# Where the operand tiles begin in SBUF: 32 bytes more among the constants, and the tiny tiles in a pool of their own at the end

## The chip, the cores and the metric

The kernel runs on one core of a Trainium2 chip. The metric is the device time of one launch, in microseconds. TensorE (PE) multiplies, its weight loads (PEld) run beside it, VectorE (DVE), ScalarE (ACT) and GpSimd (POOL) work on tiles in SBUF and PSUM, and SyncE (SP) issues nearly all DMAs. SBUF has 128 partitions; a tile takes the same stretch of bytes in each of them, and "begins at" below always means the byte within a partition.

## The reference, cut to what matters

Two blocks of two layers each run one after the other on one sequence of 256 tokens with 1024 features, all in float32.

```python
def first_block(x, ...):                     # layer 0: differential attention, layer 1: neighbourhood attention
    h = x
    for i in range(2):
        h = h + mixer_i(rmsnorm(h, norm_mix[i]))
        h = h + swiglu(rmsnorm(h, norm_ffn[i]), w_gate[i], w_up[i], w_down[i])        # hidden width 2816
        gate = sigmoid(rmsnorm(h, norm_ple[i]) @ ple_w_gate[i])
        h = h + gate * (p[i] @ ple_w_proj[i])
    return rmsnorm(h, norm_final)

def second_block(x, ...):                    # layer 0: convolution and pooling, layer 1: forgetting and block attention
    h = x
    for l in range(2):
        h = h + mixer_l(rmsnorm_2(h, mix_norm_g[l]))
        h = h + conv_ffn(rmsnorm_2(h, ffn_norm_g[l]), ...)                            # hidden width 2816
    return rmsnorm_2(h, final_norm_g)

reference = second_block(first_block(x, ...), ...)
```

The sequence is so short that the weights rule everything: some 220 MB of them are read once, and each is multiplied with 256 tokens.

## The kernel before

**Products.** Activations lie feature-major: a tile `u_both` of 128 partitions holds eight feature tiles, each with a high and a low half of 256 tokens. A float32 product is made of three matmuls on the type float32r: high by high, high by low, low by high (`mm3`). A line of the program that issues a matmul is always L195, in the helper `mm`; groups are told apart by the tile they write. The second operand named there is held in the array (stationary), the third streams through it (moving).

- `out_tile` and `pair` write `ps_g`: weights stationary, `u_both` moving, eight feature tiles of three matmuls with 256 columns.
- `wide_tile`, used by both feed-forward kinds, writes `ps_w`: for each feature tile one matmul of 512 columns (weights' high half by both halves of `u_both`) and one of 256 (weights' low half by the high half of `u_both`). The pair covers the 768 columns of an `mm3`.
- `Acc.step` writes `acc`: weights stationary, moving either `u_both` (after attention and in the mixer of the second block) or `m`, the middle of a feed-forward.
- `ps_v` has `u_both` stationary and the weights moving.
- Attention has small products (`ps_S`, `ps_V`) and transposes (`ps_t`, `ps_r`, `ps_V<-ident`), in which the tile `ident` is moving.

**Weights.** `Weights.load` sends a 512 KB piece by DMA into one of five `stage` tiles; `Weights.split` makes its high half on ACT (L88) and its low half on DVE (L89) into one of eight `w_both` tiles; `take` hands over the next one.

**Order.** Loops in Python write the program in its final order. Attention steps that would make PE wait are put off by a counter (`at`, `tick`), so that other matmuls stand between. Each engine runs its own queue in that order and waits for semaphores.

**Layout.** Pools lie one after the other in SBUF in the order in which they are opened: `const`, `stage`, `split` (the `w_both` tiles), `acts` (`u_both`) and `work`. Inside a pool tiles follow each other in the order of their first use, each size rounded up to 32 bytes. No tile is placed by hand. What this gives, worked out from the sizes in the program (the remainder on division by 512 bytes, and by 64):

| tiles | begin at, mod 512 | mod 64 |
|---|---|---|
| `h`, `ct`, `off` (in `const`) | 128, 128, 384 | 0 |
| `ident`, `tri` (in `const`) | 256 | 0 |
| `ug0`, `ug1`, `ug2` (in `const`) | 384, 416, 448 | 0, 32, 0 |
| `stage`, `w_both`, `u_both`, and of `work`: `sc`, `t2`, `bias`, `ssq`, `q`, `k`, `v`, `on` | 480 | 32 |
| `m`, `q_both`, `k_both`, `pool_m`, `R` (in `work`, behind the 32-byte tile `rstd`) | 32 | 32 |
| `a`, `sums`, `z`, `at` (in `work`, behind the 32-byte tiles `st`) | 160 | 32 |

All slices that a matmul of the large products reads begin a multiple of 512 bytes behind its tile's start, so they have the tile's remainder. One small product is an exception: `pz` has 264 columns, its moving slices of `w_both` lie 1056 bytes apart, and they begin at 480, 0 and 32 mod 512 in turn; its stationary slices of `u_both` begin at 480.

**What the change touches.** The pool list in `network` (L110 to L116), the constants (L177 on), and the places that take a tiny tile: `rstd_a` (`rstd`), `softmax_pair` and `da_steps` (`st`), `qkv_group` (`zf`), `fox_prepare` (`ft`, `lf`, `fc`).

Of the kernel before, what the change touches and what calls it, by code (L numbers as in the profile page):

```python
# [10 lines left out]
F32 = mybir.dt.float32  # L11
# [95 lines left out]
def network(ctx: ExitStack, tc: tile.TileContext, x_t, p_t, cols, b_v, na_bias, t5_bias, w_mats, out):  # L107
    nc = tc.nc

    const = ctx.enter_context(tc.tile_pool(name="const", bufs=1))  # L110
    stage = ctx.enter_context(tc.tile_pool(name="stage", bufs=N_STAGE))
    split = ctx.enter_context(tc.tile_pool(name="split", bufs=N_HI))
    acts = ctx.enter_context(tc.tile_pool(name="acts", bufs=2))
    work = ctx.enter_context(tc.tile_pool(name="work", bufs=2))
    psum = ctx.enter_context(tc.tile_pool(name="psum", bufs=1, space=PSUM))
    pass  # L116


    chunks = []
# [46 lines left out]
    for _ in range(N_STAGE - 1):  # L166
# [6 lines left out]
    dist = work.tile([128, 2, S], F32, tag="sc", bufs=3, name="dist")  # L173
    nc.gpsimd.iota(dist, pattern=[[-128, 2], [1, S]], base=0, channel_multiplier=-1,
                   allow_small_or_imprecise_dtypes=True)
    ones = const.tile([128, 1], F32, name="ones")
    nc.gpsimd.memset(ones, 1.0)  # L177
    mhalf = const.tile([128, 2], F32, name="mhalf")
# [91 lines left out]
    def rstd_a(n, eps=1e-6):  # L270
        ps = psum.tile([128, 4], F32, tag="m", bufs=2, name="ps_ss")
        two = hasattr(n, "ssq2")
        mean_square(ps[:, 0:2], n.ssq, getattr(n, "end", None))
        if two:
            mean_square(ps[:, 2:4], n.ssq2)
        st = work.tile([128, 8], F32, tag="rstd", name="rstd")
        n.rstd = st[:, 0:2]
        nc.vector.tensor_scalar(st[:, 2:4], ps[:, 0:2], 1.0 / D, eps, op0=OP.mult, op1=OP.add)  # L278
        nc.gpsimd.tensor_tensor(n.rstd, st[:, 2:4], mhalf, op=OP.pow)  # L279
        if two:  # L280

            nc.vector.tensor_mul(st[:, 4:6], n.rstd, n.rstd)
            nc.vector.scalar_tensor_tensor(st[:, 4:6], ps[:, 2:4], 1.0 / D, st[:, 4:6], op0=OP.mult, op1=OP.mult)
            nc.vector.tensor_scalar(st[:, 4:6], st[:, 4:6], eps, None, op0=OP.add)
            nc.gpsimd.tensor_tensor(st[:, 6:8], st[:, 4:6], mhalf, op=OP.pow)
            nc.vector.tensor_mul(st[:, 6:8], st[:, 6:8], n.rstd)
            n.both = st[:, 6:8]
        else:
            n.both = n.rstd
# [17 lines left out]
    def bc2(r):  # L307
        return r[:, None, :].to_broadcast([128, 2, S])
# [106 lines left out]

    def softmax_pair(sc, ps, bias, widths):

        st = work.tile([128, 8], F32, tag="st", bufs=4, name="st")
        for i in range(2):
            nc.vector.tensor_tensor_reduce(sc[:, i, :widths[i]], ps[:, i, :widths[i]], bias[i], 1.0, FLOOR,  # L420
                                           OP.add, OP.max, st[:, i:i + 1])
        nc.vector.tensor_scalar(st[:, 2:4], st[:, 0:2], -1.0, None, op0=OP.mult)  # L422
        for i in range(2):
            nc.scalar.activation(sc[:, i, :widths[i]], sc[:, i, :widths[i]], AF.Exp,  # L424
                                 bias=st[:, 2 + i:3 + i], accum_out=st[:, 4 + i:5 + i])
        nc.vector.reciprocal(st[:, 6:8], st[:, 4:6])
        return st

    def qkv_group(n, g, kind, bv, steps):
        q = work.tile([128, 2, S], F32, tag="q", bufs=1, name="q")  # L430
        k = work.tile([128, 2, S], F32, tag="k", bufs=1, name="k")

        def parts(x, tag):
            both = work.tile([128, 2, 2, S], F32R, tag=tag + "2", name=tag + "_both")
            hi = both[:, :, 0, :]
            nc.scalar.activation(hi, x, AF.Copy)
            nc.vector.tensor_sub(both[:, :, 1, :], x, hi.bitcast(F32))
            return x, both

        v = work.tile([128, 2, S], F32, tag="v", name="v")  # L440
        u = n.u
        ps = pair(u)
        if kind == "na":
            t = work.tile([128, 2, S], F32, tag="qb", bufs=1, name="qb")
            nc.vector.tensor_mul(t, ps, bc2(n.R))
            for i in range(2):
                nc.scalar.activation(q[:, i, :], t[:, i, :], AF.Identity, bias=b_q8[:, 2 * g + i:2 * g + i + 1],
                                     scale=0.125)
        else:
            nc.vector.scalar_tensor_tensor(q, ps, 0.125, bc2(n.R), op0=OP.mult, op1=OP.mult)  # L450
        q = parts(q, "q")
        ps = pair(u)
        if kind == "na":
            t = work.tile([128, 2, S], F32, tag="qb", bufs=1, name="kb")
            nc.vector.tensor_mul(t, ps, bc2(n.R))
            for i in range(2):
                nc.scalar.activation(k[:, i, :], t[:, i, :], AF.Identity, bias=col("b_k", 2 * g + i), scale=1.0)
        else:
            nc.vector.tensor_mul(k, ps, bc2(n.R))
        k = parts(k, "k")  # L460
        steps(q, k, v)
        if kind == "od" and g == 0:
            z = work.tile([128, 2, 8], F32, tag="zf", bufs=1, name="zf")
            pz = [psum.tile([128, 264], F32, tag=f"acc{2 + t}", name="pz") for t in range(2)]
            kk = 0
            for n_k in (3, 3, 2):
                w = W.take(n_k * 264)
                for i in range(n_k):
                    for t in range(2):
                        for a, b in ((0, 0), (1, 0), (0, 1)):  # L470
                            mm(pz[t], u[:, kk, a, t * 128:(t + 1) * 128], w[:, b, i * 264:(i + 1) * 264],
                               kk == 0 and (a, b) == (0, 0), kk == 7 and b == 1)
                    kk += 1
                    if kk % 2 == 0:
                        tick()
            for t in range(2):
                nc.scalar.activation(v[:, t, :], pz[t][:, :256], AF.Copy, scale=n.rstd[:, t:t + 1])
                nc.vector.scalar_tensor_tensor(z[:, t, :], pz[t][:, 256:264], n.rstd[:, t:t + 1],
                                               ct[:, COL["b_f"]:COL["b_f"] + 8], op0=OP.mult, op1=OP.add)
            fox_prepare(z, extra)  # L480
            return
        pv = psum.tile([128, 2, S], F32, tag="acc3", name="ps_v")
        for half in range(2):
            w = W.take(1024)
            for i in range(4):
                kk = 4 * half + i
                for t in range(2):
                    mm3(pv[:, t, :], u[:, kk, :, t * 128:(t + 1) * 128], w[:, :, i * 256:(i + 1) * 256],
                        kk == 0 and t == 0, kk == 7)
                if i % 2 == 1:  # L490
                    tick()
        for t in range(2):
            if kind == "na":
                nc.vector.scalar_tensor_tensor(v[:, t, :], pv[:, t, :], n.rstd[:, t:t + 1], bv,
                                               op0=OP.mult, op1=OP.add)
            else:
                nc.scalar.activation(v[:, t, :], pv[:, t, :], AF.Copy, scale=n.rstd[:, t:t + 1])
# [38 lines left out]
    def da_steps(g, q, k, v, bias, o, emitted):  # L536
        for p in range(2):
# [23 lines left out]
            def values(p=p, box=box):  # L561
                po = att_psum("V")
                at = box["at"]
                for qt in range(2):
                    for kk in range(2):
                        mm(po[:, qt * 128:(qt + 1) * 128], at[:, kk * 256 + qt * 128:kk * 256 + (qt + 1) * 128],
                           v[:, kk, p * 128:(p + 1) * 128], kk == 0, kk == 1)
                st = work.tile([128, 8], F32, tag="st", bufs=4, name="st2")
                dump = work.tile([128, 128], F32, tag="dump", bufs=1, name="dump")
                for qt in range(2):  # L570
                    nc.scalar.activation(dump, po[:, qt * 128:(qt + 1) * 128], AF.Square, accum_out=st[:, qt:qt + 1])
# [122 lines left out]
    extra = {}  # L694

    def fox_prepare(z, extra):
        zz = z.rearrange("p a b -> p (a b)")
        t = work.tile([128, 3, 16], F32, tag="ft", bufs=1, name="ft")
        nc.vector.tensor_scalar(t[:, 0, :], zz, -1.0, None, op0=OP.mult)
        nc.vector.tensor_tensor(t[:, 0, :], t[:, 0, :], zz, op=OP.min)  # L700
        nc.scalar.activation(t[:, 1, :], t[:, 0, :], AF.Exp)
        nc.scalar.activation(t[:, 1, :], t[:, 1, :], AF.Ln, bias=1.0)
        nc.vector.tensor_scalar(t[:, 2, :], zz, 0.0, None, op0=OP.min)
        lf = work.tile([128, 2, 8], F32, tag="lf", bufs=1, name="lf")
        nc.vector.tensor_sub(lf.rearrange("p a b -> p (a b)"), t[:, 2, :], t[:, 1, :])

        def cum():
            ps = psum.tile([128, 2, 8], F32, tag="m", bufs=2, name="ps_f")
            mm(ps[:, 0, :], tri, lf[:, 0, :], True, True)
            mm(ps[:, 1, :], ones.to_broadcast([128, 128]), lf[:, 0, :], True, False)  # L710
            mm(ps[:, 1, :], tri, lf[:, 1, :], False, True)
            extra["f"] = work.tile([128, 2, 8], F32, tag="fc", bufs=1, name="fc")
            nc.vector.tensor_copy(extra["f"], ps)

        cum()
# [394 lines left out]
```

## Time and profile before

| | us |
|---|---|
| median of 3 runs | 1292.58 (1291.73 to 1294.84) |
| the profiled execution's own time | 1291.94 |
| its span in the profile | 1290.1 |
| PE busy | 1260.4, 98% |
| DVE busy | 995.7, 77% |
| ACT busy | 755.1, 59% |
| POOL busy | 32.6, 3% |

The span is what the records cover; the rest of the profiled execution's time, 1.84 us, lies around it. PE is busy from start to end, with weight loads hidden beside it, so the pace at which one matmul follows another is the quantity to read. A matmul's recorded duration (280 to 400 ns) is longer than that pace, since matmuls overlap in the pipeline; the pace comes from the chain of work that ended last, which names for each run of matmuls its start, its length up to the next piece, and its count: length by count is the pace. Where a row of the timeline gives a run of n matmuls, its length holds n - 1 paces and one full duration. Columns of float32r at TensorE's full clock of 2.4 GHz take 0.4167 ns each, 256 of them 106.7 ns, 768 of them 320 ns, if one goes in per cycle.

### The profile page before, as it was taken

Reading aid. Unit: us, or ns where it says so; the run is one execution under the profiler, and the core shown is the slowest. Engines: PE = TensorE matmul, PEld = TensorE weight load, DVE = VectorE, ACT = ScalarE, POOL = GpSimd, SP = SyncE. Lnnn points to the kernel's source line nnn. Section 1 sums busy time; section 2 is a strip of 40 time slices with the busy share of each in tenths; the row PEclk is TensorE's granted clock in tenths of the full one; section 3 lists DMA queues with packets and bytes.
Section 4 is the critical chain, followed back from the end, with each engine's and each line's share of the span. In section 5 each row is a group of like instructions: output and inputs, shape, how many; then the busy total and the mean of one; then the engine's idle time right before and its main releaser. Section 6 shows DMA issues by size and latency. Waiting matters only on the chain.

```text
span 1290.1 us, 23187 instructions
## 1 busy us (share of the span) xinstructions
PE 1260.4 (98%) x9040; PEld 1165.1 (90%) x9040; DVE 995.7 (77%) x1884; ACT 755.1 (59%) x1354; POOL 32.6 (3%) x54
## 2 busy tenths in 40 slices
PE   6999999999999999999999999999999999999997
PEld 6999899999989998999999998999999898899997
DVE  7876877777876667777788889888886766888884
ACT  6776655555666565555567456555665565655563
POOL 1000000000010000000000000000000000000000
PEclk9999999999999999999999999999999999999998
DMA  8554666664757436566546475666645343566640
GB/s 281 157 160 147 186 191 193 191 183 147 230 167 189 130 116 213 192 191 187 180 140 204 127 244 168 191 187 191 186 151 192 99 131 131 180 193 185 193 133 34
DMA packets 62926, 222.30 MB, mean 172 GB/s; under 512 B 7264, under 2 KB 7776, under 8 KB 62688
## 3 DMA queue, kind: packets, MB, share of 16 engines
q1 hardware_dynamic: 60768, 214.52, 53.6%
q0 software_dynamic: 1616, 5.77, 1.9%
q8 instruction: 71, 1.16, 0.4%
q10 hardware_dynamic: 432, 0.53, 0.1%
q14 instruction: 39, 0.32, 0.1%
HBM read 219.74 MB, written 1.05 MB: 171 GB/s over the span
## 4 chain that ended last, share of the span: by engine, by line
PE 91%; DVE 4%; issue 1%; POOL 1%; DMA 1%; ACT 1%; SPq 0%; POOLq 0%; DVEq 0%; ACTq 0%
PE ps_w L195 36%; PE acc L195 24%; PE ps_g L195 16%; PE ps_v L195 5%; PE ps_S L195 3%; PE ps_V L195 2%; PE ps_t L394 1%; DVE w_both L89 1%; DVE u_both L256 1%; PE ps_p L195 1%; POOL rstd L279 1%; DVE h L372 1%; DVE ssq L247 1%; DMA stage<-w_da_qkv 1%; ACT w_both L88 1%
## 5 line engine op out<-in xcount | busy, mean ns | idle before, releaser
L89 DVE TENSOR_TENSOR w_both<-stage,w_both 128x1024 fp32r<-128x1024 f32 (+2 forms) x413 | 495.3, 1201 | 123.8 <-ACT w_both L88 122.1
L88 ACT ACTIVATE w_both<-stage 128x1024 fp32r<-128x1024 f32 (+2 forms) x413 | 427.7, 1037 | 174.8 <-issue 55.3
L195 PE MATMUL ps_w<-u_both,w_both 128*128 128x512 f32 (+1 forms) x2816 | 504.4, 339 | 1.0 <-DVE u_both L256 1.0
L195 PEld LDWEIGHTS ps_w<-u_both,w_both 128*128 128x128 f32 x2816 | 431.1, 189 | 63.7 <-DVE u_both L256 2.3
L195 PE MATMUL ps_g<-u_both,w_both 128*128 128x256 f32 x1920 | 254.0, 289 | 8.0 <-ACT w_both L88 7.5
L195 PE MATMUL acc<-m,w_both 128*128 128x256 f32 x2112 | 255.8, 280 | 0.0
L195 PEld LDWEIGHTS acc<-m,w_both 128*128 128x128 f32 x2112 | 251.5, 188 | 1.8
L195 PEld LDWEIGHTS ps_g<-u_both,w_both 128*128 128x128 f32 x1920 | 238.5, 193 | 12.3 <-ACT w_both L88 7.5
L340 ACT ACTIVATE sums<-ps_w 128x256 f32<-128x256 f32 x176 | 67.6, 384 | 197.0 <-PE ps_w L195 197.0
L341 DVE TENSOR_TENSOR sums<-ps_w,sums 128x256 f32<-128x256 f32 x176 | 74.2, 422 | 54.1 <-ACT sums L340 53.7
L195 PE MATMUL acc<-u_both,w_both 128*128 128x256 f32 x768 | 98.2, 286 | 0.4 <-DVE u_both L585 0.4
L195 PEld LDWEIGHTS acc<-u_both,w_both 128*128 128x128 f32 x768 | 93.8, 192 | 2.1 <-DVE u_both L585 0.6
L195 PE MATMUL ps_v<-w_both,u_both 128*128 128x256 f32 x528 | 70.7, 287 | 0.0
L195 PEld LDWEIGHTS ps_v<-w_both,u_both 128*128 128x128 f32 x528 | 65.4, 191 | 3.3 <-issue 1.5
L424 ACT ACTIVATE sc<-sc,st 128x256 f32<-128x256 f32 (+1 forms) x96 | 46.0, 482 | 17.2 <-DVE st L422 17.2
L731 ACT ACTIVATE t<-sums 128x256 f32<-128x256 f32 x88 | 36.6, 416 | 18.4 <-DVE sums L762 15.0
L254 ACT ACTIVATE u_both<-h,ct 128x256 fp32r<-128x256 f32 x72 | 32.3, 497 | 16.7 <-DVE h L372 14.9
L734 DVE SCALAR_TENSOR_TENSOR t<-t,sums 128x256 f32<-128x256 f32 x88 | 37.4, 425 | 2.8
L279 POOL TENSOR_TENSOR rstd<-rstd,mhalf 128x2 f32<-128x2 f32 x11 | 12.2, 1105 | 1079.3 <-DVE rstd L278 1079.3
L735 ACT ACTIVATE m<-t 128x256 fp32r<-128x256 f32 x88 | 35.7, 406 | 3.5 <-DVE t L734 3.4
L256 DVE SCALAR_TENSOR_TENSOR u_both<-h,ct,u_both 128x256 fp32r<-128x256 f32 x72 | 31.6, 480 | 7.9 <-ACT u_both L254 7.9
L736 DVE TENSOR_TENSOR m<-t,m 128x256 fp32r<-128x256 f32 x88 | 36.9, 419 | 1.0 <-ACT m L735 1.0
(164 smaller groups left out, 843.2 us busy)
## 6 DMA issues: line engine op xcount, KB each, us to landing
stage<-w_gu SPq DMA_DIRECT2D x88, 512.0 KB, 3.7
stage<-w_in SPq DMA_DIRECT2D x88, 512.0 KB, 4.0
stage<-w_down SPq DMA_DIRECT2D x44, 512.0 KB, 3.7
stage<-w_out SPq DMA_DIRECT2D x44, 512.0 KB, 4.1
stage<-w_na_qkv SPq DMA_DIRECT2D x24, 512.0 KB, 4.6
stage<-w_da_qkv SPq DMA_DIRECT2D x23, 512.0 KB, 4.9
stage<-w_od_in SPq DMA_DIRECT2D x22, 512.0 KB, 4.2
stage<-w_gate SPq DMA_DIRECT2D x16, 512.0 KB, 3.6
```

The source lines that it names most:

```text
L88: self.nc.scalar.activation(hi[:, s], t[:, s], AF.Copy)
L89: self.nc.vector.tensor_sub(lo[:, s], t[:, s], hi[:, s].bitcast(F32))
L195: nc.tensor.matmul(o, a, b, start=start, stop=stop, **kw)
L254: nc.scalar.activation(n.u[:, 2 * b + i, 0, :], src[:, i, :], AF.Copy, scale=gain(2 * b + i))
L256: nc.vector.scalar_tensor_tensor(n.u[:, 2 * b + i, 1, :], src[:, i, :], gain(2 * b + i), n.u[:, 2 * b + i, 0, :].bitcast(F32), op0=OP.mult ...
L340: nc.scalar.activation(out, ps[:, 1, :], AF.Copy)
L341: nc.vector.tensor_add(out, ps[:, 0, :], out)
L424: nc.scalar.activation(sc[:, i, :widths[i]], sc[:, i, :widths[i]], AF.Exp, bias=st[:, 2 + i:3 + i], accum_out=st[:, 4 + i:5 + i])
L731: nc.scalar.activation(t, g, AF.Tanh, scale=0.5)
L734: nc.vector.scalar_tensor_tensor(mf, a, 0.5, other, op0=OP.mult, op1=OP.mult)
L735: nc.scalar.activation(m[:, 0, :], mf, AF.Copy)
L736: nc.vector.tensor_sub(m[:, 1, :], mf, m[:, 0, :].bitcast(F32))
```

## The change

A 32-byte tile `pad` is added among the constants and filled with zeros, and nothing reads it. With it the constants end 32 bytes later, at a multiple of 512 bytes, and so `stage`, `w_both`, `u_both` and `work` begin there. The tiles of 32 to 192 bytes leave `work` for a new pool `small` behind it, with the same tags and numbers of buffers. All larger tiles of `work` then begin at multiples of 512 bytes. The constants behind `pad` move by 32 bytes: `ident` and `tri` from 256 to 288 mod 512, `ug0`, `ug1`, `ug2` from 384, 416, 448 to 416, 448, 480. `h`, `ct` and `off` stay.

```diff
@@ network
     work = ctx.enter_context(tc.tile_pool(name="work", bufs=2))
+    small = ctx.enter_context(tc.tile_pool(name="small", bufs=2))
     psum = ctx.enter_context(tc.tile_pool(name="psum", bufs=1, space=PSUM))
-    pass
...
+
+    pad = const.tile([128, 8], F32, name="pad")
+    nc.gpsimd.memset(pad, 0.0)
     ones = const.tile([128, 1], F32, name="ones")
     nc.gpsimd.memset(ones, 1.0)
@@ rstd_a
-        st = work.tile([128, 8], F32, tag="rstd", name="rstd")
+        st = small.tile([128, 8], F32, tag="rstd", name="rstd")
@@ softmax_pair
-        st = work.tile([128, 8], F32, tag="st", bufs=4, name="st")
+        st = small.tile([128, 8], F32, tag="st", bufs=4, name="st")
@@ qkv_group
-            z = work.tile([128, 2, 8], F32, tag="zf", bufs=1, name="zf")
+            z = small.tile([128, 2, 8], F32, tag="zf", bufs=1, name="zf")
@@ da_steps
-                st = work.tile([128, 8], F32, tag="st", bufs=4, name="st2")
+                st = small.tile([128, 8], F32, tag="st", bufs=4, name="st2")
@@ fox_prepare
-        t = work.tile([128, 3, 16], F32, tag="ft", bufs=1, name="ft")
+        t = small.tile([128, 3, 16], F32, tag="ft", bufs=1, name="ft")
...
-        lf = work.tile([128, 2, 8], F32, tag="lf", bufs=1, name="lf")
+        lf = small.tile([128, 2, 8], F32, tag="lf", bufs=1, name="lf")
...
-            extra["f"] = work.tile([128, 2, 8], F32, tag="fc", bufs=1, name="fc")
+            extra["f"] = small.tile([128, 2, 8], F32, tag="fc", bufs=1, name="fc")
```

The order of instructions and their waits on PE, DVE, ACT and SP is the same in both programs. Only POOL's queue gets one instruction more, near its start. POOL before, from the second iota to the first DMA:

```order
8 L174 IOTA dist 128x512
9 L177 MEMSET ones 128x1
10 L179 MEMSET mhalf 128x2
11 L181 MEMSET zero_102 128x16
12 L183 IOTA rcnt 128x64
```

POOL after, the same stretch:

```order
8 L174 IOTA dist 128x512
9 L178 MEMSET pad 128x8
10 L180 MEMSET ones 128x1
11 L182 MEMSET mhalf 128x2
12 L184 MEMSET zero_107 128x16
13 L186 IOTA rcnt 128x64
```

The memset of `pad` stands ahead of `ones`; everything behind it on POOL comes one place later and is otherwise unchanged.

## Rows read from the trace of the kernel before

**Rows 1.** The page's part 1: busy time, share of the span, instructions by engine.
```profile
PE 1260.4 (98%) x9040; PEld 1165.1 (90%) x9040; DVE 995.7 (77%) x1884; ACT 755.1 (59%) x1354; POOL 32.6 (3%) x54
```

**Rows 2.** Waits of PE, the longest in total: microseconds, times, longest.
```profile
PE ps_r L295 <- POOL rstd L279: 8.3, 9, 2.5
```

**Rows 3.** Groups of PE's matmuls, shapes apart: count, busy, mean ns, idle before.
```profile
L195 PE MATMUL ps_w<-u_both,w_both 128*128 128x512 f32 x1408 | 497.8, 398 | 1.0 <-DVE u_both L256 1.0
L195 PE MATMUL ps_w<-u_both,w_both 128*128 128x256 f32 x1408 | 392.8, 280 | 0.0
L195 PE MATMUL acc<-m,w_both 128*128 128x256 f32 x2112 | 255.8, 280 | 0.0
L195 PE MATMUL ps_g<-u_both,w_both 128*128 128x256 f32 x1920 | 254.0, 289 | 8.0 <-ACT w_both L88 7.5 <-DVE w_both L89 0.5
L195 PE MATMUL acc<-u_both,w_both 128*128 128x256 f32 x768 | 98.2, 286 | 0.4 <-DVE u_both L585 0.4
L195 PE MATMUL ps_v<-w_both,u_both 128*128 128x256 f32 x528 | 70.7, 287 | 0.0
...
L195 PE MATMUL ps_V<-v,at 128*128 128x128 f32 x64 | 8.6, 278 | 0.0
...
L394 PE MATMUL ps_t<-ident,a 128*128 128x128 f32 x32 | 5.1, 272 | 0.0
```

**Rows 4.** Chain that ended last, pieces in order: start us, length us, what xcount.
```profile
152.07 5.44 PE acc L195 x48
...
202.33 5.66 PE acc L195 x48
207.98 11.11 PE ps_w L195 x64
...
523.46 11.30 PE ps_w L195 x64
...
716.72 15.95 PE ps_g L195 x133
732.67 1.18 PE ps_pool L195 x10
...
753.14 15.86 PE acc L195 x132
```

**Rows 5.** The same chain, asked for 488.6 to 491.3 alone.
```profile
488.59 2.96 PE ps_w L195 x9
```

**Rows 6.** Three stretches, PE alone: length, busy (count), granted clock, DMA share, GB/s.
```profile
488.60:491.20 2.60, 2.60 (x9) 0.50 0.72 208
...
720.00:733.00 13.00, 13.00 (x111) 1.00 0.15 50
...
753.00:769.00 16.00, 16.00 (x136) 1.00 0.79 246
```

**Rows 7.** Timeline of PE: start us, length us, a run of equal matmuls.
```profile
70.30 0.60 PE L394 MATMUL ps_t<-ident,a 128*128 128x128 f32 x4
...
75.26 1.06 PE L195 MATMUL ps_V<-v,at 128*128 128x128 f32 x8
```

**Rows 8.** The same view, 967 to 982: matmuls of 264 columns.
```profile
976.29 5.82 PE L195 MATMUL pz<-w_both,u_both 128*128 128x264 f32 x47
```

**Rows 9.** Timeline of ACT at L772; the first reads `ug0`, the second `ug1`.
```profile
804.35 0.60 ACT L772 ACTIVATE sums<-ug,ct 128x256 f32<-128x256 f32 x1
...
838.02 0.60 ACT L772 ACTIVATE sums<-ug,ct 128x256 f32<-128x256 f32 x1
```

**Rows 10.** Busy time by stretch: length, PE, PEld, DVE, ACT, POOL, clock, DMA share.
```profile
783.00:962.00 179.00, 178.74 (x1199) 163.90 (x1200) 152.31 (x267) 107.13 (x178) 0.20 (x1) 1.00 0.62 187
```

**Rows 11.** Timeline of POOL at the start: start us, length us, instruction, idle before.
```profile
1.65 0.10 POOL L177 MEMSET ones<- 128x1 f32 x1
...
21.22 3.36 POOL L279 TENSOR_TENSOR rstd<-rstd,mhalf 128x2 f32<-128x2 f32 x1 [18.50 <-DVE rstd L278]
```

**Rows 12.** The chain again, its first long DMA.
```profile
6.45 7.74 DMA stage<-w_da_qkv
```

## The prediction

> **What bounds the kernel now.** I read the busy shares first: PE is busy 98% of the span [rows 1]. Then PE's waits: the longest kind adds up to 8.3 us [rows 2]. So what the change can move is the pace of the matmuls, and the groups say which: six of them hold 8,144 matmuls on float32r (1,408 + 1,408 + 2,112 + 1,920 + 768 + 528) [rows 3]. The chain gives their pace, length by count [rows 4]. `ps_g` needs 15.95 / 133 = 119.9 ns for 256 columns, `acc` from `u_both` 15.86 / 132 = 120.2, `acc` from `m` 5.66 / 48 = 117.9, once 5.44 / 48 = 113.3; a `ps_w` pair of 512 and 256 columns needs 11.11 / 32 = 347.2, in one feed-forward 11.30 / 32 = 353.1. The bare columns at 2.4 GHz are 106.7 and 320 ns.
>
> Put over the same 768 columns (three matmuls of 256, or one pair), these are 360, 353, 340, 347 and 353 ns. Sixteen columns take 6.67 ns at 2.4 GHz and are 64 bytes of float32 in a partition; in that unit the five are 54.0, 53.0, 51.0, 52.1 and 53.0, against 48 that the columns need. That they come out so near whole numbers is why I read the pace as counted in pieces of 64 bytes; it is a reading, not a row. At the lower clock nothing is lost: where the granted clock was 0.50 [rows 6], nine matmuls of the same kind took 2.96 us [rows 5]. Four pairs of 0.64 us, which is 768 columns at 1.2 GHz, and 0.40 us for the last one's own length make that.
>
> What lies above the bare columns: 3,216 matmuls (`ps_g`, `acc` from `u_both`, `ps_v`) at 13.3 ns are 43 us; 2,112 at 11.1 are 23 us; 1,056 pairs (three feed-forwards) at 27.2 and 352 (one) at 33.1 are 29 + 12 us. In all **107 us**; with PE's waits, that is all the change could ever give.
>
> **The change part by part.** The memset of `pad` is one POOL instruction of about 0.10 us, by that of `ones` [rows 11]. Behind it stand memsets, an iota and the issue of one DMA for the second layer's attention; POOL's next computation starts at 21.22 us after 18.50 us of waiting for DVE [rows 11]. The wait for DVE hides it: 0; without that cover 0.1 us. The tiny tiles keep tags and buffers, so no wait is added or removed: 0.
>
> The DMAs into `stage` now begin at a multiple of 512 bytes. The transfers land beside PE's work except at the start, where the chain holds 7.74 us of them [rows 12]. I take 0; if a better start made them a tenth faster, 0.8 us less, and the reverse if slower.
>
> DVE and ACT: the same ACT instruction takes 0.60 us from `ug0`, which begins at 0 mod 64, and from `ug1`, which begins at 32 [rows 9]. I take 0 for all their 3,200 instructions.
>
> The matmuls are what is left. Before, each stream of the large products starts at 32 mod 64, so 1,024 bytes touch 17 pieces of 64 bytes and 2,048 bytes touch 33; after, 16 and 32. *Lower bound of the gain*: nothing, since at the lower clock the same misplaced streams cost nothing [rows 5] and ACT doesn't care [rows 9]. *Upper bound of this mechanism*: one piece for each matmul, 6.67 ns x 8,144 = 54 us. The nearest row between: 128-column runs of float32, where the moving tile is `v` at 32 mod 64 or `ident` at 0 mod 64. Eight matmuls from `v` took 1.06 us, less one duration of 278 ns [rows 3, 7]: 0.782 / 7 = 111.7 ns. Four from `ident` took 0.60, less 272 [rows 3, 7]: 0.328 / 3 = 109.3. The difference is 2.4 ns for a matmul, though one is a product and the other a transpose, and the timeline's hundredths leave some 2 ns of doubt. I take 2.4 ns, the only row that compares the two starts on PE: 2.4 x 8,144 = **19.5 us less**. `ident` moves to 32 mod 64, so some 230 transposes may pay the 2.4 ns that the others save: 0.5 us more.
>
> What is late next: DVE is busy 152.31 of 179 us in the densest feed-forward [rows 10], 85%; with PE 1.5% faster it is 86%, so it doesn't bind. The clock fell to half at the start of this one feed-forward [rows 6], for about 3 us; if shifted work brings one such fall more or less, that is 1.5 us either way.
>
> Sum, against the profiled execution's own 1291.94 us (0.6 under the median of the three runs): 1291.94 - 19.5 + 0.5 = 1272.9, rounded to **1273**.
>
> [...] A matmul of 256 columns is paced at 118 to 120 ns [rows 4]. [...] The trace has no block of 256 columns below 113.3 ns [rows 4], so this end gets 0.04, inside the chance of the whole piece below.
>
> **Rivals.**
>
> *A whole piece.* Each stream gives back the full 64-byte piece: 1291.94 - 54 = 1238. For it: the best block of `acc`, 113.3 ns, is 17.0 pieces [rows 4], just what a misplaced stream touches; and `pz`, with 264 columns, is paced at (5.82 - 0.28) / 46 = 120.4 ns [rows 8], no slower than 256 columns, as if both were counted in whole pieces (17 for either). Against: 17 pieces can as well be 16 and one lost at each change of weights, in which case the start is innocent.
>
> *No change.* The pace is set by the handing over of weights and its rhythm, not by where tiles start. For it: the same addresses gave 113.3 and 117.9 ns in `acc`, 347 and 353 in `ps_w` [rows 4]; ACT doesn't care [rows 9]; and the pace was 120 with the DMAs at 15% and at 79% [rows 4, 6], so it isn't SBUF traffic. Time 1292. [...]
>
> *Slower.* The distance between the two operands counts, not the start itself. `m` and `pool_m` begin at 32 mod 512, their weights at 480: 64 bytes apart. Those run at 117.9 and 1.18 / 10 = 118 ns; `ps_g` and `acc` from `u_both`, where both begin at 480, run at 120 [rows 4]. After the change all begin at 0, so `acc` from `m` would fall to 120: 2.2 ns x 2,112 = 4.6 us more, 1296.6, and one more fall of the clock makes 1298. It decides from the point where equal remainders cost 2 ns and the start costs nothing. Against: in `pz` the distance is 0, 32 and 64 bytes in turn, at one pace of 120.4 [rows 8].
>
> **How the numbers follow.** A measurement of this kernel can tell about 0.3%, 4 us, from no change. Chances: my forecast, a part of a piece (1250 to 1288), 0.33; a whole piece or more (below 1250) 0.17; no change (1288.7 to 1296.5) 0.27; slower 0.23. So faster 0.50, same 0.27, slower 0.23. The likeliest single case is the forecast, 1273. The range has to reach over no change and the 1298 of the slower rival, and down to the whole piece with a few microseconds of the start: 1236 to 1298. What lies below and above these holds 0.2 at most.
>
> **What would show it.** In the chain after, `ps_g` near 117.5 ns and `acc` from `m` near 115.5, a `ps_w` pair 5 ns shorter, and the order of waits as before: the forecast. `ps_g` at 113.3 and a pair at 333 to 340: the whole piece. `ps_g` still 120.0 and `ps_w` 347 or 353: no change, and 120 in `acc` from `m` beside it: the slower rival. Transposes from `ident` at 111 to 112 ns would confirm that the start of the moving tile is what counts. A longer time with unchanged paces would mean that a wait or the clock, which I priced at 1.5 us, has moved, and the argument by pace would be wrong.

## The result, and the profile after

The changed kernel takes 1301.86 us, median of four runs (1298.08 to 1302.84); the kernel before, run beside it, 1292.93 (1291.73 to 1294.84). The ratio is 1.0062, with a 95% interval of 1.0039 to 1.0086: slower by 0.6%, 8.9 us, and above the upper end of the forecast's range. The profiled execution is the fastest of the four, 1298.08 us with a span of 1296.3; that of before had 1291.94 and 1290.1. The traces therefore have 6.2 us of span to explain, and the other 3 us of the medians are not in them.

The first question is whether an engine or a wait has moved. Part 1 of the page, then PE's waits (total us, times, longest), both of the changed kernel:

```profile
PE 1267.5 (98%) x9040; PEld 1170.2 (90%) x9040; DVE 996.6 (77%) x1884; ACT 754.6 (58%) x1354; POOL 32.7 (3%) x55
```

```profile
PE ps_r L298 <- POOL rstd L282: 8.3, 9, 2.5
PE ps_g L198 <- ACT w_both L88: 6.9, 1, 6.9
PE ps_ss L198 <- DVE half L266: 3.7, 5, 0.8
```

Against [rows 1], DVE and ACT are within 1 us of where they were, POOL has its one memset more, and PE alone has grown, by 7.1 us. The longest kind of wait is 8.3 us as in [rows 2]. Nothing waits longer; the matmuls have become slower.

Which ones, the groups say (count, busy us, mean ns of one, idle before). Lines are 3 higher than in [rows 3].

```profile
L198 PE MATMUL ps_w<-u_both,w_both 128*128 128x512 f32 x1408 | 500.2, 399 | 1.1 <-DVE u_both L259 1.0
L198 PE MATMUL ps_w<-u_both,w_both 128*128 128x256 f32 x1408 | 394.4, 281 | 0.0
L198 PE MATMUL acc<-m,w_both 128*128 128x256 f32 x2112 | 260.7, 283 | 0.0
L198 PE MATMUL ps_g<-u_both,w_both 128*128 128x256 f32 x1920 | 253.2, 288 | 7.6 <-ACT w_both L88 6.9 <-DVE w_both L89 0.7
L198 PE MATMUL acc<-u_both,w_both 128*128 128x256 f32 x768 | 98.2, 286 | 0.4 <-DVE u_both L588 0.4
L198 PE MATMUL ps_v<-w_both,u_both 128*128 128x256 f32 x528 | 70.7, 287 | 0.0
```

`acc` from `u_both` and `ps_v` have to the tenth what they had in [rows 3], and `ps_g` is 0.8 us lower. What has grown is `acc` from `m`, by 4.9 us, and the two halves of `ps_w`, by 2.4 and 1.6. The chain gives the paces behind that (start us, length us, what); these are whole pieces of the changed kernel:

```profile
25.32 5.76 PE ps_v L198 x48
...
202.51 5.75 PE acc L198 x48
208.26 11.31 PE ps_w L198 x64
...
507.09 11.31 PE ps_w L198 x64
...
718.31 15.95 PE ps_g L198 x133
```

`ps_g` runs at 15.95 / 133 = 119.9 ns, as in [rows 4]. `acc` from `m` runs at 5.75 / 48 = 119.8 where it had 117.9, and a `ps_w` pair at 11.31 / 32 = 353.4 where this stage had 347.2. The start is better by a little: the first block of `ps_v` begins at 25.32 us where before it began at 26.14.

Taken over all of a group, from start to start of its matmuls in the trace, with falls of the clock and waits left out, the paces in ns are (before, then after): `ps_g` 119.7 and 119.7, `acc` from `u_both` 119.8 and 119.8, `ps_v` 119.7 and 119.7, `acc` from `m` 117.6 and 119.9, a `ps_w` pair 346.9 and 353.3 in most blocks of three feed-forwards (272, 272 and 304 pairs of the 352 in each, 848 in all), 353.2 and 353.3 in the second.

One more thing differs. The stretches in which the granted clock was at half (0.50) in the trace of before (columns: length, PE's busy time and count, granted clock, DMA share, GB/s; first before, then after):

```profile
488.00:491.40 3.40, 3.40 (x12) 0.50 0.73 234
1099.00:1102.40 3.40, 3.40 (x13) 0.50 0.64 206
```

```profile
488.00:491.40 3.40, 2.30 (x14) 1.00 0.47 159
1099.00:1102.40 3.40, 2.27 (x14) 1.00 0.57 175
```

Inside both falls the `ps_w` pairs of before follow each other at 640 ns from start to start, 427 behind the 512 columns and 213 behind the 256: 0.833 ns for a column. If the pace goes with the granted clock, that is 0.417 ns at the full one; the 2.4 GHz, 106.7 and 320 ns of the prediction stand as an estimate from this, and no row at the full clock shows them.

Before had two such falls ahead of its last microseconds, the profiled execution of after had none. At the prediction's 1.5 us each that gives back 3.0 us. The account of the span:

| term | us |
|---|---|
| `acc` from `m`: 2,112 x (119.90 - 117.62) ns | +4.8 |
| `ps_w`: the 848 pairs that ran at 346.9 ns, x 6.4 ns | +5.4 |
| two falls of the clock fewer | -3.0 |
| the first block earlier | -0.8 |
| sum | +6.4 |
| measured, span | +6.2 |

The other runs of after were granted 0.994 of the full clock over their span, the profiled one 0.997; they took 3.6 to 4.8 us more. That is the size of two or three such falls, but they have no trace that shows them.

### The profile page after: what moved, and what is told of

Read it like the earlier page. It is cut to its first block, busy times and chain, and to the rows that moved or that the text cites. A ratio compares the mean times of both kernels' runs of the same rounds, so it can differ in the third digit from the quotient of the medians.

```text
span 1296.3 us, 23188 instructions
## 1 busy us (share of the span) xinstructions
PE 1267.5 (98%) x9040; PEld 1170.2 (90%) x9040; DVE 996.6 (77%) x1884; ACT 754.6 (58%) x1354; POOL 32.7 (3%) x55
## 4 chain that ended last, share of the span: by engine, by line
PE 90%; DVE 5%; issue 1%; POOL 1%; ACT 1%; DMA 0%; POOLq 0%; DVEq 0%; ACTq 0%
PE ps_w L198 37%; PE acc L198 25%; PE ps_g L198 16%; PE ps_v L198 5%; PE ps_S L198 3%; PE ps_V L198 2%; DVE w_both L89 2%; PE ps_t L397 1%; DVE u_both L259 1%; PE ps_p L198 1%; POOL rstd L282 1%; DVE h L375 1%; DVE ssq L250 1%; PE ps_ss L198 0%; ACT w_both L88 0%
## 5 line engine op out<-in xcount | busy, mean ns | idle before, releaser
L198 PE MATMUL acc<-m,w_both 128*128 128x256 f32 x2112 | 260.7, 283 | 0.0
L198 PEld LDWEIGHTS acc<-m,w_both 128*128 128x128 f32 x2112 | 256.3, 192 | 2.0
```

The lines of the kernel that those rows point to most:

```text
L198: nc.tensor.matmul(o, a, b, start=start, stop=stop, **kw)
```

## The experiments

Two explanations stood against each other. *The start*: a moving tile at 32 mod 64 costs something that one at 0 doesn't. *The distance*: what counts is how far apart, mod 512, the starts of the two operands of a matmul lie, the moving tile and the weights; the start itself costs nothing. The change moves all large tiles by the same 32 bytes except `m`, which moves by 480 (from 32 to 0). So it leaves the distance of `u_both` to its weights at 0 and takes that of `m` from 64 to 0. The twelve runs set starts and distances apart. Their places, mod 512, and the paces from their traces, in ns over all of each group (`ps_w`: most blocks of a feed-forward). In e7, e10 and e11 the tile of `u_both` is 128 bytes longer than in the others, so the second of its two buffers begins 128 bytes further on than the first (given behind the semicolon), and `m`, which lies behind both buffers, 256 bytes further on:

| kernel | weights | `u_both` | `m` | `ps_g` | `acc` from `m` | `ps_w` pair |
|---|---|---|---|---|---|---|
| before | 480 | 480 | 32 | 119.7 | 117.6 | 346.9, in one 353.2 |
| after | 0 | 0 | 0 | 119.7 | 119.9 | 353.3 |
| e1_pad_only | 0 | 0 | 64 | 119.7 | 117.6 | 346.9, in one 353.2 |
| e2_small_only | 480 | 480 | 480 | 119.7 | 119.9 | 353.3 |
| e3_u64 | 0 | 64 | 64 | 117.5 | 117.8 | 353.4 |
| e4_u256 | 0 | 256 | 256 | 119.7 | 119.9 | 353.3 |
| e5_u128_m32 | 0 | 128 | 32 | 118.8 | 117.1 | 350.4 to 351.1 |
| e6_u32_m96 | 0 | 32 | 96 | 117.2 | 119.9 | 347.1 |
| e7_two_starts | 0 | 0 and 64; 128 and 192 | 320 | 117.3 at 64, 114.9 at 192 | 117.8 | 353.2 at 0, 351.2 at 128 |
| e8_m_low_64 | 0 | 0 | 64 (high half) | 119.7 | 117.6 | 346.9 |
| e9_u32_m32 | 0 | 32 | 32 | 116.9 | 116.7 | 346.7 |
| e10_u16_m48 | 0 | 16; 144 | 304 | 117.1 at 16, 118.5 at 144 | 118.3 | 346.6 to 347.1 |
| e11_u48_m16 | 0 | 48; 176 | 272 | 118.3 at 48, 119.3 at 176 | 118.6, in one feed-forward 116.6 | 346.6 at 48, 349.9 at 176 |
| e12_no_pad | 480 | 0 | 0 | 116.9 | 116.7 | 346.7 |

### The two parts of the change, apart

The first kernel has only the 32 bytes among the constants; the tiny tiles stay where they were. The second has only the pool at the end.

```diff
 e1_pad_only, against the kernel before:
+    pad = const.tile([128, 8], F32, name="pad")
+    nc.gpsimd.memset(pad, 0.0)

 e2_small_only, against the changed kernel:
-    pad = const.tile([128, 8], F32, name="pad")
-    nc.gpsimd.memset(pad, 0.0)
```

> Only the 32-byte tile is added; the tiny tiles stay in `work`. Weights and `u_both` begin at 0 mod 512, `m` at 64. Theory of distance (weights and moving tile beginning at the same remainder cost `acc` from `m` about 2 ns a matmul, and its rhythm slows `ps_w` too): `acc` from `m` back at 117.8 ns, a `ps_w` pair at 347 in three of the four feed-forwards, time 1292 to 1294. Theory of the start (a start at a multiple of 64 or 512 bytes is what costs): `acc` from `m` stays at 120, pairs at 353, time 1298 to 1302.

> Only the tiny tiles move; no 32-byte tile. Weights, `u_both` and `m` all begin at 480 mod 512, so at 32 mod 64 as before the change, but with no distance between them. Theory of distance: `acc` from `m` at 120, `ps_w` pairs at 353 everywhere, time 1298 to 1302. Theory of the start: as before the change, 117.8 and 347, time 1292 to 1294.

Measured: with the 32 bytes alone 1290.9 us against 1289.78, ratio 1.0009 (0.9998 to 1.0021), no change that can be told. With the pool alone 1301.22, ratio 1.009 (1.0065 to 1.0114), as slow as the whole change. The chain of the first, then of the second:

```profile
203.16 5.66 PE acc L197 x48
208.81 11.11 PE ps_w L197 x64
...
522.76 11.30 PE ps_w L197 x64
```

```profile
204.42 5.75 PE acc L196 x48
210.17 11.31 PE ps_w L196 x64
```

What follows: the first has every large tile at a multiple of 64 bytes and runs like the kernel before, row by row, even to the one feed-forward at 11.30 us. The second has them all at 32 mod 64 and runs like the changed kernel. The start on a 64-byte boundary is worth nothing that can be told; the tiny tiles' move, which brings `m` to its weights' remainder, is worth the whole loss.

### Another distance for `u_both`

If the distance counts, `u_both` is the tile to move, since 3,216 matmuls of 256 columns and all of `ps_w` read it at distance 0. A tile in a pool of its own ahead of `acts` puts all that lies behind it 64 or 256 bytes further.

```diff
 against the changed kernel:
+    gap_u = ctx.enter_context(tc.tile_pool(name="gap_u", bufs=1))
     acts = ctx.enter_context(tc.tile_pool(name="acts", bufs=2))
 ...
+    gu = gap_u.tile([128, 16], F32, name="gu")      # e3_u64: 16; e4_u256: 64
+    nc.gpsimd.memset(gu, 0.0)
```

> The changed kernel with a 64-byte tile between the weights and `u_both`: weights at 0, `u_both` and `m` at 64 mod 512. Theory of distance: `acc` from `m` at 117.8, and now `ps_g`, `ps_v` and `acc` from `u_both` leave 120 for 118 as well, 3,216 matmuls by 2 ns or 6 to 7 us less than before the change, time 1284 to 1288. Theory of the start: all at 120 as in the changed kernel, 1298 to 1302. If only `m` follows the distance and `u_both` doesn't: 1292 to 1294.

> The same with a tile of 256 bytes: `u_both` and `m` at 256 mod 512, weights at 0. Theory of distance: a pace other than 120 in every group of 256 columns; if any distance does, 118 ns and 1284 to 1288; if it counts how far the two operands' reads run apart, lower than at 64 bytes, down to the 113.3 ns once seen in `acc`, which would be 1240 to 1270. Theory of the start: 120 and 1298 to 1302.

Measured: 1294.49 us with 64 bytes, ratio 1.0038 (1.0023 to 1.0054); 1300.22 with 256, ratio 1.0082 (1.0062 to 1.0103). Both are still slower than before. The chain of the first, then of the second:

```profile
203.72 5.65 PE acc L201 x48
209.37 11.31 PE ps_w L201 x64
...
717.50 15.66 PE ps_g L201 x133
```

```profile
203.84 5.75 PE acc L201 x48
209.59 11.31 PE ps_w L201 x64
...
721.13 15.95 PE ps_g L201 x133
```

At 64 bytes `ps_g` takes 15.66 / 133 = 117.7 ns where it took 119.9, and `acc` from `m` is back at 117.7; at 256 bytes all is as at 0. So the distance works on `u_both` as it does on `m`. But the time missed the 1284 to 1288 that I had worked out for 64 bytes: the 3,216 matmuls gave some 8 us (2.2 to 3.7 ns each), while `ps_w` stayed at 353 in the three feed-forwards that before has mostly at 347, which costs 5.4 us, and the profiled run had four falls of the clock where before's had two. Together these come to less than 1 us more, and the profiled span is 2.9 us longer than before's, so some 2 us of it stay open. For `ps_w`, then, 64 bytes are no better than 0, and what it does is not read off the matmuls of 256 columns.

### Each tile at a distance of its own

Two kernels with `u_both` and `m` at different distances, set by one more such pool ahead of `work`.

```diff
 against the changed kernel, in sizes of the two tiles:
+    gu = gap_u.tile([128, 32], F32, name="gu")      # e5_u128_m32: 32, 104; e6_u32_m96: 8, 16
+    gm = gap_m.tile([128, 104], F32, name="gm")
```

> Weights at 0, `u_both` at 128, `m` at 32 mod 512. If the distance counts modulo 128 bytes: `ps_g`, `ps_v` and `acc` from `u_both` at 120 as for a distance of 0 and 256, with `ps_w` at 353. If it counts modulo 256 or 512: below 120, like 64 bytes or better. `acc` from `m` at a distance of 32 bytes: between, some 119, if it goes with how far the reads lie apart; 120 or 117.8 if whole 64-byte pieces count.

> Weights at 0, `u_both` at 32, `m` at 96 mod 512. The same question with the groups exchanged: `ps_g` and the others from `u_both` show a distance of 32, `acc` from `m` one of 96. If 64-byte pieces of the address count, 32 goes with 0 (120) and 96 with 64 (117.8), or the streams that begin inside a piece pay for it and both lie at 120. `ps_w` pairs 347 or 353; the theory has no say there.

Measured, in a single run each: 1293.86 and 1294.65 us. The chain of the second:

```profile
204.26 5.76 PE acc L204 x48
210.02 11.11 PE ps_w L204 x64
...
508.61 11.11 PE ps_w L204 x64
...
753.69 15.41 PE acc L204 x132
```

With `u_both` at 32 the 132 matmuls of `acc` that read it take 15.41 us, 116.7 ns each, where they took 15.86 [rows 4], and `ps_w` is at 347 in the second feed-forward too, where none of the kernels so far had it. With `m` at 96, `acc` from `m` is at 120.0, as at distance 0. The other kernel adds that `m` at 32 has 117.1 and `u_both` at 128 has 118.8. The single times say little: the profiled run of e6 had five falls of the clock, that of e5 two, one of them 6.8 us long.

### Is it one pace or a rhythm?

Two kernels ask whether a group's pace belongs to its own two operands alone. The first gives `u_both` distance 0 where a feed-forward reads it and 64 elsewhere, by a view into a larger tile, and puts `m` at 320. The larger tile makes four distances of the two: the second buffer of `u_both` begins 128 bytes further on, so the last feed-forward reads it at 128 and several of the other stages at 192. The second puts only the low half of `m` 64 bytes further (so the high half is at 64 and the low half at 128), and leaves `ps_w` and all else as in e1.

```diff
 e7_two_starts, against e1_pad_only:
-    def split_act(tag="u"):
-        return acts.tile([128, KT, 2, S], F32R, tag=tag, name="u_both")
+    def split_act(far=True):
+        t = acts.tile([128, KT * 2 * S + 32], F32R, tag="u", name="u_both")
+        o = 16 if far else 0
+        return t[:, o:o + KT * 2 * S].rearrange("p (k a s) -> p k a s", k=KT, a=2)

 e8_m_low_64, against e1_pad_only:
-            m = work.tile([128, 2, S], F32R, tag=("q2", "k2")[j % 2], name="m")
+            m = work.tile([128, 2, S + 16], F32R, tag=("q2", "k2")[j % 2], name="m")[:, :, :S]
```

> Weights at 0, `m` at 64 mod 128, and `u_both` begins at 0 mod 128 where a feed-forward reads it and at 64 elsewhere. Theory of distance: `acc` from `m` 117.8; `ps_g`, `ps_v`, `acc` from `u_both` 117.5 instead of 119.8, 3,216 x 2.3 = 7 us less than before the change; `ps_w` as before the change, 347 in three feed-forwards. Time 1283 to 1287, faster than both kernels. If `ps_w` doesn't come back to 347: 1290 to 1293.

> The kernel with only the 32-byte tile, and the low half of `m` 64 bytes further: the high half at 64, the low half at 0 mod 128 from the weights. If each stream pays for itself, `acc` from `m` lies a third of the way from 117.8 to 120, at 118.5. If the rhythm of the three is one, it is 117.8 or 120 as a whole (or a new value), and the `ps_w` pairs go with it: 347 with the former, 353 with the latter.

Measured: e7 takes 1286.16 us (1282.21 to 1293.59), ratio 0.9946 (0.9926 to 0.9965); e8 takes 1288.98 in its single run. Pieces of the chain, first of e7, where the second line is read at 0, the third (a `ps_g` block behind the first feed-forward) at 192, the fourth at 64 and the last at 128; then that `ps_g` block in e3, at 64; then e8:

```profile
203.26 5.65 PE acc L197 x48
208.91 11.30 PE ps_w L197 x64
...
339.25 5.46 PE ps_g L197 x48
...
716.03 15.67 PE ps_g L197 x133
...
1184.72 11.24 PE ps_w L197 x64
```

```profile
339.89 5.65 PE ps_g L201 x48
```

```profile
203.34 5.65 PE acc L197 x48
208.99 11.10 PE ps_w L197 x64
505.88 11.10 PE ps_w L197 x64
```

What follows: `ps_w` in e8 has the same instructions at the same addresses as in e1, and in the second feed-forward it runs at 11.10 us where e1 has 11.30. So a pace is not fixed by the two addresses alone; at distance 0 it can take one of two values, and the only thing altered is where the low half of `m` lies, which the `acc` blocks in between read. Inside those, the single streams of e8 lie at 118.2, 115.2 and 119.8 ns (high by high, high by low, low by high), where e1 has 117.6, 117.4 and 117.9. Only the second kind reads the moved half, and what it gains the other two give back: 353.2 ns for the three, 352.9 in e1.

In e7 `ps_w` runs at 353 again in the three feed-forwards that read `u_both` at distance 0, though `acc` from `m` is at 117.8 beside it; in the last, at 128, it has 11.24 / 32 = 351.3, near e5. `ps_g` has 117.3 at 64, as in e3, and 114.9 at 192, lower than any group at any other distance, which I had not set out to test. The time of e7 lies in the 1283 to 1287 expected, but by luck: that sum wanted `ps_w` back at 347, which did not come, and the stages at 192, which it did not have, gave more instead. Its profiled run, 1293.59 us with five falls of the clock, is the slowest of its six; the other five took 1282.21 to 1287.04, and without a trace of those it stays open whether the clock alone makes that.

### 32 bytes for both

> The changed kernel with a 32-byte tile between the weights and `u_both`: weights at 0, `u_both` and `m` at 32 mod 512. By the paces that the two kernels before it showed at a distance of 32 bytes: `ps_g` and `acc` from `u_both` 117, `ps_v` 118, `ps_w` pairs 347 in all four feed-forwards, `acc` from `m` 117. Against the kernel before the change: 1,920 x 2.6 + 768 x 2.9 + 528 x 1.4 ns = 8 us, one feed-forward of 352 pairs x 6.2 = 2 us, 2,112 x 0.6 = 1 us: 1279 to 1284. If the paces of one group depend on the distance of the other: 1286 to 1292. A start inside a 64-byte piece (theory of the start) would make it 1298 or more.

It is the changed kernel with the tile `gu` at 8 floats (32 bytes), as in e3. Measured: 1280.69 us (1279.14 to 1282.49), inside the 1279 to 1284 expected, ratio 0.992 (0.9903 to 0.9937). Its chain:

```profile
201.54 5.60 PE acc L201 x48
207.14 11.09 PE ps_w L201 x64
...
501.79 11.09 PE ps_w L201 x64
...
745.12 15.41 PE acc L201 x132
```

All groups are at their best at once: 5.60 / 48 = 116.7 ns, 11.09 / 32 = 346.6 for a pair in all four feed-forwards, 15.41 / 132 = 116.7.

### 16 and 48 bytes

Half that step, by a view that starts 4 floats (`u_both`) or 12 floats (`m`) inside a larger tile, and the two exchanged.

```diff
 e10_u16_m48, against the changed kernel (e11_u48_m16: 12 and 4 in place of 4 and 12):
+    def split_act(o=4):
+        t = acts.tile([128, KT * 2 * S + 32], F32R, tag="u", name="u_both")
+        return t[:, o:o + KT * 2 * S].rearrange("p (k a s) -> p k a s", k=KT, a=2)
 ...
+            m = work.tile([128, 2 * S + 32], F32R, tag=("q2", "k2")[j % 2], name="m")
+            m = m[:, 12:12 + 2 * S].rearrange("p (a s) -> p a s", a=2)
```

> Weights at 0, `u_both` 16 bytes further, `m` 48. Open: whether the pace goes evenly with the distance (`ps_g` between 117 and 120, some 118.4; `acc` from `m` 117 to 118) or has a best place. `ps_w` pairs 347 or 353.

> The reverse: `u_both` 48 bytes further than the weights, `m` 16. Evenly: `ps_g` 117 to 117.5, `acc` from `m` 118.4, `ps_w` pairs between the 347 of 32 bytes and the 353 of 64.

Here too the second buffer begins 128 bytes further on, so each kernel mixes two distances of `u_both`: 16 and 144 in e10, 48 and 176 in e11; `m` lies at 304 and 272. Measured: 1287.65 and 1288.15 us in a single run each. `ps_w` is near 347 in both but for the last feed-forward of e11, which reads `u_both` at 176; the matmuls of 256 columns lie between those at 0 and at 32, `ps_g` with 117.1 to 119.3. In that last feed-forward of e11 `acc` from `m` changes as well, from 118.6 to 116.6, with its own addresses as they were. Its blocks in the first feed-forward and in the last:

```profile
202.57 5.69 PE acc L198 x48
...
1207.88 5.60 PE acc L198 x48
```

So of the distances that all three kinds were given, 32 is the best; `ps_g` alone was faster at 192 (e7), where `ps_w` was not tried.

### The same addresses for what streams, other ones for the weights

The last run is the sharpest between the two explanations. It is e9 without `pad`: `u_both` and `m` begin at 0 mod 512, exactly where the changed kernel has them, and only the weights and `stage` lie at 480 again.

```diff
 against the changed kernel:
+    gap_u = ctx.enter_context(tc.tile_pool(name="gap_u", bufs=1))
     acts = ctx.enter_context(tc.tile_pool(name="acts", bufs=2))
 ...
-    pad = const.tile([128, 8], F32, name="pad")
-    nc.gpsimd.memset(pad, 0.0)
+    gu = gap_u.tile([128, 8], F32, name="gu")
+    nc.gpsimd.memset(gu, 0.0)
```

> The kernel of the 32-byte tile before `u_both`, without the 32-byte tile among the constants: `u_both`, `m` and the rest of `work` begin at 0 mod 512, just where the changed kernel has them, and only the weights (and `stage`) begin 32 bytes earlier, at 480. Theory of distance: the paces and the time of the kernel with the 32-byte tile, `ps_g` 117, `ps_w` 347, `acc` from `m` 117, 1279 to 1284. If it matters that the weights begin at 0 and the moving tiles at 32: something else, up to the changed kernel's 120, 353 and 1298 to 1302.

Measured: 1279.48 us (1278.6 to 1280.96) against 1291.12, ratio 0.9906 (0.9892 to 0.992). The chain:

```profile
201.71 5.60 PE acc L199 x48
207.31 11.09 PE ps_w L199 x64
...
745.38 15.41 PE acc L199 x132
```

The moving tiles begin where those of the changed kernel begin, and every group runs as in e9, at 116.7 ns and 346.6. Between this kernel and the changed one lie 32 bytes in the place of the weights and 22 us of their medians, though the two were not run side by side. It beats both kernels, by 0.9% and 1.7%, at the price of one memset and 32 bytes in a partition.

## Why the prediction failed

**The bound was right.** PE stayed at 98% busy, the order of the waits stayed, and the whole difference lies in the paces of the six groups, the falls of the clock and 0.8 us at the start. DVE and ACT moved by under 1 us. The start improved by 0.8 us, the figure that the text had for transfers into `stage` that land a tenth faster; the chain there no longer goes through them, so it isn't shown that they are the cause.

**The step that failed is the 2.4 ns for each matmul.** It was the difference of two rows, eight products from `v` at 32 mod 64 and four transposes from `ident` at 0 [rows 7], put down to the start of the moving tile. After the change both have exchanged places: `v` begins at 0 and `ident` at 32 mod 64. The timeline of the changed kernel:

```profile
69.49 0.60 PE L397 MATMUL ps_t<-ident,a 128*128 128x128 f32 x4
...
74.46 1.06 PE L198 MATMUL ps_V<-v,at 128*128 128x128 f32 x8
```

0.60 and 1.06 us, as in [rows 7]. So the start does not make the 2.4 ns. That one is a transpose and the other a product, the doubt that the text itself named, is what is left: the program issues 32 products from `v`, and [rows 3] has 64 records of them, two for each, but 32 for the 32 transposes from `ident`. With that falls 19.5 us of gain; in its place the runs showed nothing for the start (e1: all large tiles at multiples of 64 bytes, ratio 1.0009) and 2.3 ns more for each `acc` matmul from `m`. The test that the text set, transposes from `ident` at 111 to 112 ns, came out against it. The reading of the paces as whole pieces of 64 bytes, on which the rival of a whole piece rested, falls with it: e1 has no stream that straddles a piece more than it must, and its paces are those of before. No run shows the paces under 113.3 ns that got 0.04: over all runs no large group was below 116.0 ns on the whole, and `ps_g` taken at 192 alone (e7) had 114.9.

**The slower rival had the mechanism, and was argued away by one wrong reading.** It said that the distance counts and that `acc` from `m` would go to 120 ns; it went to 119.9. Its price was 4.6 us, measured 4.8. It got 0.23 because `pz`, whose weights' slices lie at distances of 0, 32 and 64 in turn, shows one pace of 120.4 [rows 8]. That row hardly reacts to the distances. The changed kernel, with the same three, and e3_u64, where each is 64 bytes less:

```profile
980.73 5.82 PE L198 MATMUL pz<-w_both,u_both 128*128 128x264 f32 x47
```

```profile
978.24 5.87 PE L201 MATMUL pz<-w_both,u_both 128*128 128x264 f32 x47
```

5.87 us is 121.5 ns for each against 120.4, where `ps_g` became 2.2 ns faster. In `pz` the weights stream and `u_both` is held, the columns are 264, and the distance changes within the run; e8 shows that what one stream gains its neighbours can give back, so such a mixture says little of its parts. It was weak evidence, and with a steadier row, `ps_g` at 120 and `acc` from `m` at 118 in one trace [rows 4], the rival was the better reading.

**What nobody's sum had is `ps_w`.** The rival left it out, and neither of its operands changes its distance. It went to 353 in all feed-forwards: 848 pairs x 6.4 ns = 5.4 us, more than `acc` itself. A warning stood in [rows 4]: one feed-forward at 353 with the same addresses. In the trace of before there is a second: the first blocks of the first feed-forward also run at the slow pace, while `acc` between them has 113.3, and then the pace tips over (start, length, what, in the chain of before):

```profile
157.51 11.31 PE ps_w L195 x64
168.82 5.66 PE acc L195 x48
```

So the pace of `ps_w` at distance 0 is one of two that it can hold, and something beside its own addresses decides which: in e8 it was the place of the low half of `m`. With this term the rival comes to 1291.94 + 4.8 + 5.4 = 1302.1 us, or 1298.3 with the -3.8 us of falls and start that this one execution happened to have; the profiled one took 1298.08 and the median is 1301.86. The range ended at 1298 because it allowed one fall of the clock and no second group.

**No change** rested on the same addresses giving two paces; that is so (e8), but it doesn't exclude that addresses matter as well. For the starts alone it held (e1, ratio 1.0009), for the distances it did not (e9, 0.992).

**What stays open.** Why a distance of 0 costs 3 ns against 32, and why 256 is as 0 while 64 lies near 32 and 96 at 0 again, is not shown: the runs show only that the pace depends on the distance. It isn't the distance of a group's own two operands alone either: in e11 `acc` from `m` goes from 118.6 to 116.6 with its addresses unchanged. What tips `ps_w` from 353 to 347 is shown only to be something in its neighbours. And the number of falls of the clock, none to five in the profiled runs, is not tied to anything that I varied; it blurs single times by some 7 us (five at the estimate of 1.5 us), which is why paces, and not times, carry the verdicts where there is a single run.

## What to carry to other kernels

When PE is the bound and its pace lies above the bare columns, look at where the two operands of a matmul lie relative to each other, not at round addresses: here 32 bytes between the remainders mod 512 of weights and moving tile were worth 0.9%, and making all equal cost 0.6%. Moving all tiles alike by 32 bytes changed nothing here that can be told (e1, ratio 1.0009); list the distances before and after, and ask which group is the only one whose distance alters. Before trusting a small difference between two rows, find two rows that differ in that one thing, and if a trace shows one group at two paces with the same addresses, price its slower pace into the range.

## What the runs showed of the hardware that I had not expected

- Float32r matmuls of 256 columns with a new weight tile each ran at 119.7 to 119.9 ns at distances of 0 and 256 bytes, 119.9 at 96, 118.8 at 128, 117.0 to 117.8 at 64 and 116.7 to 117.2 at 32 (`ps_v`, where the weights stream, is in the next point). `ps_g` had 117.1 at 16, 118.3 at 48, 118.5 at 144, 119.3 at 176 and 114.9 at 192.
- The sign of the distance, or which tile streams, counts a little (the two were not set apart): `ps_v`, where the weights stream and `u_both` is held, has 118.1 in e12 while `ps_g` has 116.9; in e3, at 64 bytes, it is the other way round, 116.0 against 117.5.
- The same `ps_w` instructions at the same addresses ran steadily at 346.9 ns a pair in one kernel (e8) and at 353.2 in another (e1), through a whole feed-forward but for its first blocks.
- A start at 0 or at 32 mod 64 made no difference that can be told: e1 to before 1.0009 in time, ACT 754.6 us after and 755.1 before, DVE 996.6 and 995.7, transposes 0.60 us for four either way.
